# Two-layer hybrid encoder: a unit's transposes alternate on TensorE with the former unit's products with the values

## The chip, the cores and the metric

The kernel runs on one core of one Trainium2 chip. The metric is the time of one execution on the device in microseconds (us), the median of the runs. A profile of one execution comes with it; its times are us from the start of the span.

## What is computed

The reference is one step of a streaming encoder with two layers. Each layer adds to its input an output projection of three groups of heads side by side, and then an MLP. The first group is latent attention (MLA, 6 heads, each chunk of 64 frames sees all earlier chunks), the second a gated linear attention (GLA, 4 heads), the third attention over a band of chunks (6 heads, each chunk sees itself and the 8 before it). There are 1024 prompt frames and 8 running streams with 16 new frames each, 1152 columns in all; everything is float32.

```python
def _ca_prompt(q, k, v, table):
    ...
    s = jnp.einsum('bnqhe,bnkhe->bnhqk', qc, kb).astype(f32) * (E ** -0.5)
    ...
    p = jax.nn.softmax(s, axis=-1).astype(v.dtype)
    return jnp.einsum('bnhqk,bnkhe->bnqhe', p, vb).reshape(B, S, H * E)
...
for l in range(DEPTH):
    q, ckv, kr, gq, gk, gv, loga, g_out, cq, ck, cv = _project(_rmsnorm(xp, norm1[l]), pos_p, *proj_w)
    k_m, v_m = _mla_kv(ckv, kr, mla_w_kvup[l])
    o_mla = _mla_prompt(q, k_m, v_m)
    o_gla, S_fin = _gla_prompt(gq, gk, gv, loga)
    o_ca = _ca_prompt(cq, ck, cv, ca_rel_bias[l])
    xp = xp + _merge(o_mla, o_gla, g_out, o_ca, gla_out_norm[l], w_out[l])
    xp = xp + _mlp(_rmsnorm(xp, norm2[l]), w_up[l], w_down[l])
```

## The kernel before

A float32 value is kept as a high and a low part of a narrower type, and a product of two such values is made of up to three TensorE products (high by high, high by low, low by high). The dense projections work on columns in three groups of 384; each of their products is a "z" in the profile (128x384).

A layer runs through these stages (of layer 0, in us): norm and first input projections to 70; band attention 70 to 367; gated linear attention 367 to 545; latent attention 545 to 772; its sample part 772 to 810; norm, then the MLP 855 to 1618. Layer 1 repeats them: band attention 1688 to 1985, latent attention 2163 to 2385. In the attention stages two streams are merged. The primary stream is the attention; the dense stream, called the filler here, is the rest of the input projection and parts of the output projection. `drive()` (L358) takes from the one or the other in proportion to their costs, which each generator yields as it goes, so that TensorE has dense products while other engines do the softmax. The primary stream is emitted at a higher priority. From what is emitted, a scheduler sets the order on each engine by its own estimate of when operands are ready; the filler's products have scheduling-only dependencies on each other (`fq`, L58 to L63), which tie an order and wait for nothing at run time.

The function that the change touches is `attention()` (L395), which both attention stages use. Its unit is one head and two query tiles of 128, `a` = 0 and 1. For each query tile:

- `s_step` (L399) makes the scores with `mm` (L57) in one or two banks "s", takes the row maximum on DVE (L408), the exponent on ACT (L413) and normalises on DVE (L417). In band attention the operands of a score have 64 partitions ("64*128" in the profile, kH and qH), in latent attention 96.
- `t_step` (L420) runs three query tiles behind (`lag`). It transposes the probabilities on TensorE (`tr`, L72) block by block, up to four blocks of 128x128 into a bank "tp" (tile `ptp`). ACT copies the bank to the high part of a tile PT (L151), and DVE subtracts that from the bank to make the low part (L135). A bank is free once DVE has read it. PT tiles of the first four key blocks have two buffers, those of the later ones have one. GpSimd clears blocks that only one of the query tiles sees (L433).
- `pv_step` (L450) comes once for a unit, after both query tiles: it multiplies the values by all PT tiles into a bank "pv", first all high parts, then all low ones, in the order of the key blocks, up to 16 products in a row (128x256 each). ACT copies the bank out and the result is stored.

The loop at the end of `attention()` emits for each query tile its scores, then the whole `pv_step` of a unit that is pending, then the `t_step` of the query tile three behind. The eight PSUM banks are cut as d 2, s 2, tp 2, pv 2 in band attention, and d 2, s 3, tp 2, pv 1 in latent attention ("d" holds the filler's products).

## Time and profile before

| what | value |
|---|---|
| median of 3 runs | 3263.82 us (3259.57 to 3268.15) |
| profiled execution, its span | 3266.2 us |
| TensorE (PE) busy | 3137.7 us, 96% |
| VectorE (DVE), ScalarE (ACT), GpSimd (POOL) busy | 56%, 36%, 27% |
| span of a band attention stage, of a latent one | 297 us; 227 us (layer 0), 222 us (layer 1) |

For the profiled execution the span is its own time; it lies within the spread of the three runs. A row of a timeline has the start, the time from the first instruction's start to the last one's end, engine, line, operation, the tile written and the tiles read, shapes, and how many alike follow each other. Matmuls are pipelined, so the time of one row overlaps the next: the pace is read from start to start. The windows view gives the busy time of each engine in a stretch. PEld is TensorE's loading of the stationary operand.

### The profile page before, as it was taken

The numbers are of one execution on the slowest core, as the hardware profiler recorded it, in microseconds if no ns is written. First come the engines' busy times: TensorE is split into PE (matmuls) and PEld (weight loads), VectorE is DVE, ScalarE is ACT, GpSimd is POOL, SyncE is SP. The second block draws the span as 40 slices with busy tenths as digits, with TensorE's granted clock in tenths as the row PEclk, the third lists the DMA queues.
The fourth block names the chain that finished last, engine by engine and source line by source line (L and its number), as shares of the span: only waits on it lengthen the run. The fifth ranks groups of instructions, "written<-read, shape, count | busy, mean of one in ns | idle before, by whom it ended". The sixth has DMA issues, their size and how long they took to land.

```text
span 3266.2 us, 49236 instructions
## 1 busy us (share of the span) xinstructions
PE 3137.7 (96%) x18652; PEld 2982.4 (91%) x18652; DVE 1834.2 (56%) x3785; ACT 1190.6 (36%) x2781; POOL 866.1 (27%) x1122
## 2 busy tenths in 40 slices
PE   8999998998999999999999999889999999999998
PEld 7888887887999999999989888878889999999998
DVE  4554687885734434434555646978855443434436
ACT  4443454774311121111244434557743121111122
POOL 5221355443310010100242214654532010010112
PEclk9999999989999999999999999999999999999998
DMA  5232215224011111111143222142331111111111
GB/s 182 86 100 78 88 50 159 67 83 149 30 43 46 39 46 40 46 39 46 62 140 105 85 74 86 57 150 75 111 104 39 46 40 46 40 46 45 40 46 59
DMA packets 137612, 237.67 MB, mean 73 GB/s; under 512 B 16768, under 2 KB 105056, under 8 KB 137376
## 3 DMA queue, kind: packets, MB, share of 16 engines
q1 hardware_dynamic: 137376, 234.53, 22.3%
q8 instruction: 147, 2.41, 0.3%
q14 instruction: 89, 0.73, 0.1%
HBM read 178.64 MB, written 55.84 MB: 72 GB/s over the span
## 4 chain that ended last, share of the span: by engine, by line
PE 82%; DVE 9%; ACT 4%; issue 3%; DMA 1%; POOL 1%; SPq 0%; DVEq 0%; ACTq 0%; POOLq 0%
PE z L57 67%; PE s L57 4%; PE pv L57 3%; PE ptp L72 2%; PE rb L57 1%; DVE ga L743 1%; PE glao L57 1%; DVE mq L734 1%; PE lev L57 1%; DVE sbd L796 1%; ACT P L413 1%; DVE M L729 1%; PE ms L57 0%; DVE ng L408 0%; ACT PT L151 0%
## 5 line engine op out<-in xcount | busy, mean ns | idle before, releaser
L57 PE MATMUL z<-u,wdnh 128*128 128x384 f32 x3072 | 712.9, 334 | 0.1
L57 PEld LDWEIGHTS z<-u,wdnh 128*128 128x128 f32 x3072 | 548.6, 188 | 0.4 <-DVE u L135 0.4
L1253 DVE TENSOR_TENSOR x<-z,x 128x384 f32<-128x384 f32 x720 | 364.5, 551 | 288.0 <-PE z L57 288.0
L1227 POOL TENSOR_TENSOR relu<-relu 128x384 f32<-128x384 f32 x192 | 166.7, 895 | 1340.8 <-ACT u L1226 1336.1
L57 PE MATMUL z<-u,wdnl 128*128 128x384 f32 x1536 | 445.9, 334 | 0.0
L57 PE MATMUL z<-hH,wupl 128*128 128x384 f32 x1536 | 373.3, 334 | 0.0
L57 PE MATMUL z<-hL,wuph 128*128 128x384 f32 x1536 | 373.1, 334 | 0.0
L57 PE MATMUL z<-hH,wuph 128*128 128x384 f32 x1536 | 372.2, 334 | 0.0
L146 ACT ACTIVATE wdnh<-wdnr 128x1024 fp32r<-128x1024 f32 x64 | 68.0, 1062 | 686.4 <-PE z L57 686.4
L57 PEld LDWEIGHTS z<-u,wdnl 128*128 128x128 f32 x1536 | 282.3, 188 | 0.0
L57 PEld LDWEIGHTS z<-hH,wupl 128*128 128x128 f32 x1536 | 275.8, 188 | 0.0
L57 PEld LDWEIGHTS z<-hL,wuph 128*128 128x128 f32 x1536 | 275.8, 188 | 0.0
L57 PEld LDWEIGHTS z<-hH,wuph 128*128 128x128 f32 x1536 | 275.7, 188 | 0.0
L146 ACT ACTIVATE wuph<-wupr 128x1024 fp32r<-128x1024 f32 x64 | 68.0, 1062 | 514.6 <-PE z L57 512.6
L135 DVE TENSOR_TENSOR wdnl<-wdnr,wdnh 128x1024 fp32r<-128x1024 f32 x64 | 78.1, 1221 | 302.7 <-ACT wdnh L146 302.7
L135 DVE TENSOR_TENSOR wupl<-wupr,wuph 128x1024 fp32r<-128x1024 f32 x64 | 78.2, 1221 | 205.8 <-ACT wuph L146 205.8
L413 ACT ACTIVATE P<-s,ng 128x320 f32<-128x320 f32 (+5 forms) x288 | 157.4, 552 | 85.8 <-DVE ng L410 59.1
L135 DVE TENSOR_TENSOR u<-relu,u 128x384 fp32r<-128x384 f32 x192 | 148.9, 801 | 50.9 <-POOL relu L1227 50.9
L135 DVE TENSOR_TENSOR PT<-ptp,PT 128x512 fp32r<-128x512 f32 (+3 forms) x288 | 146.0, 518 | 52.6 <-ACT PT L151 44.3
L151 ACT ACTIVATE PT<-ptp 128x512 fp32r<-128x512 f32 (+3 forms) x288 | 127.3, 460 | 126.1 <-PE ptp L72 116.5
L72 PE MATMUL ptp<-ident,P 128*128 128x128 f32 x792 | 139.9, 283 | 15.2 <-DVE PT L135 12.0
L408 DVE TENSOR_REDUCE ng<-s 128x1 f32<-128x320 f32 (+5 forms) x288 | 146.7, 516 | 7.0 <-PE s L57 2.7
(416 smaller groups left out, 6447.5 us busy)
## 6 DMA issues: line engine op xcount, KB each, us to landing
wupr<-in_w_up_dram SPq DMA_DIRECT2D x64, 512.0 KB, 3.3
wdnr<-in_w_down_dram SPq DMA_DIRECT2D x64, 512.0 KB, 3.3
zs_dram<-z SPq DMA_DIRECT2D x102, 192.0 KB, 1.9
wo1r<-in_w_out_dram SPq DMA_DIRECT2D x48, 320.0 KB, 3.0
of<-os_dram SPq DMA_DIRECT2D x48, 192.0 KB, 3.5
xpart_dram<-xo SPq DMA_DIRECT2D x48, 192.0 KB, 1.9
xo<-xpart_dram SPq DMA_DIRECT2D x48, 192.0 KB, 3.5
cf<-zs_dram SPq DMA_DIRECT2D x36, 192.0 KB, 4.3
```

The lines of the kernel that those rows point to most:

```text
L57: i = T.matmul(*a, **k).ins
L72: T.transpose(out, in_, idn)
L135: eng.tensor_tensor(lo, src, h.bitcast(F32), ALU.subtract)
L146: S.activation(h, raw, AF.Copy)
L151: S.activation(o, i, AF.Copy, scale=scale)
L408: V.tensor_reduce(ng[:, x:x + 1], sc[x][:, :hi - lo], AX.X, ALU.max, negate=True)
L413: S.activation(pr[:, lo:hi], sc[x][:, :hi - lo], AF.Exp, bias=ng[:, 0:1], accum_out=ss[:, x:x + 1])
L729: V.tensor_tensor(mv[:, :, 0, :], mv[:, :, 0, :], kv[:, :, 0, :], ALU.mult)
L734: (GP if h else V).tensor_tensor(q2[hr, h, :w // 2].rearrange("p (n s) -> p n s", s=s), mv[hr, :, 1, :], qv[hr, :, 1, :], ALU.mult)
L743: V.copy_predicated(o, mk.to_broadcast([P, 2 * nt, 64 // s, s]), src)
L1227: GP.tensor_tensor(r, r, r, ALU.mult)
L1253: V.tensor_tensor(x[:, gsl(g)], o, x[:, gsl(g)], ALU.add)
```

## The change

Three things change in `attention()` and the helpers under it; no instruction is added or removed.

First, `pv_step` becomes a generator that stops after each product, and its products come in another order: the last four key blocks first, then the four before them; within four blocks all high parts, then all low ones.

Second, `t_step` calls `between()` ahead of each transpose, which emits the next product or products of the former unit. Under the first query tile these are half of the unit's products, under the second the rest, spread over the transposes. Before the next unit's generator starts, what is left of the former is emitted.

Third, transposes and products emitted in this way are tied to one another, each to the one before it, by a scheduling-only dependency (`behind`), so that the scheduler keeps them in this alternating order on TensorE.

```diff
+    def behind(i):
+        if chain:
+            tc.add_manual_dep(i, chain[0], NOSYNC, reason="order")
+        chain[:] = [i.name]
...
     def mm(*a, **k):
         i = T.matmul(*a, **k).ins
+        if linked[0]:
+            behind(i)
...
     def tr(out, in_, idn):
-        T.transpose(out, in_, idn)
+        i = T.transpose(out, in_, idn).ins
+        if linked[0]:
+            behind(i)
...
-            def t_step(u, a, pr):
+            def t_step(u, a, pr, between):
...
                     for i in range(n):
+                        linked[0] = True
+                        between(a, u.nk(a) - j - i)
                         tr(tp[:, i * P:(i + 1) * P], pr[:, (j + i) * P:(j + i + 1) * P], ident)
+                        linked[0] = False
...
             def pv_step(u):
                 po = bank("pv", "pv")
-                for w in range(2):
-                    for j in range(u.nj):
-                        mm(po[:, :256], u.v(u.jlo + j), u.pt[j // 4][w][:, j % 4, :],
-                           start=(w == 0 and j == 0), stop=(w == 1 and j == u.nj - 1))
+                todo = [(j, w) for x in reversed(range(0, u.nj, 4)) for w in range(2) for j in range(x, min(x + 4, u.nj))]
+                for i, (j, w) in enumerate(todo):
+                    mm(po[:, :256], u.v(u.jlo + j), u.pt[j // 4][w][:, j % 4, :],
+                       start=i == 0, stop=i == len(todo) - 1)
+                    if i < len(todo) - 1:
+                        yield
...
+            pend = [None, 0, 0]
+            def advance(n):
+                for _ in range(n):
+                    if pend[0] is not None:
+                        pend[1] -= 1
+                        if next(pend[0], "end") == "end":
+                            pend[0] = None
+            def between(a, left):
+                n = pend[1] if a else pend[1] - pend[2]
+                advance(-(-n // left))
+            def t_and_pv():
+                u, a, pr = todo.pop(0)
+                n = pend[1]
+                yield from t_step(u, a, pr, between)
+                yield (n - pend[1]) * 109
+                if a == 1:
+                    yield pend[1] * 109
+                    advance(99)
+                    pend[:] = [pv_step(u), 2 * u.nj, u.nj]
...
                     todo.append((u, a, s_step(u, a)))
                     yield u.nk(a) * P * u.npass / 2.4
-                    if pend is not None:
-                        pv_step(pend)
-                        yield pend.nj * 218
-                        pend = None
                     if len(todo) > lag:
-                        yield from t_step(*todo[0])
-                        if todo[0][1] == 1:
-                            pend = todo[0][0]
-                        todo.pop(0)
+                        yield from t_and_pv()
```

The lines of the file move with it: `mm` stands at L65 after, `tr` at L82.

On TensorE, in band attention of layer 0, at the second unit of the first pair of heads, before: `s` are scores from kH, kL, qH and qL, `pv` the products with values `cvhl`, `z` the filler.

```order
L57 MATMUL s_1869<-kH_1454,qH_1452 128x256
L57 MATMUL s_1869<-kL_1455,qH_1452 128x256
L57 MATMUL s_1869<-kH_1454,qL_1453 128x256
L57 MATMUL pv_1722<-PT_1693,cvhl_773 128x256
L57 MATMUL pv_1722<-PT_1693,cvhl_774 128x256 x2
L57 MATMUL pv_1722<-PT_1695,cvhl_774 128x256 x2
L57 MATMUL s_1881<-kH_1454,qH_1452 128x256
L57 MATMUL s_1881<-kL_1455,qH_1452 128x256
L57 MATMUL s_1881<-kH_1454,qL_1453 128x256
L57 MATMUL z_1913<-hH_380,win15h_1741 128x384
```

The same place after (`ptp` are the transposes of P):

```order
L65 MATMUL pv_1656<-PT_1573,cvhl_774 128x256
L82 MATMUL ptp_1711<-ident,P_1566 128x128
L65 MATMUL pv_1656<-PT_1573,cvhl_774 128x256
L82 MATMUL ptp_1711<-ident,P_1566 128x128
L65 MATMUL s_1869<-kH_1444,qH_1442 128x256
L65 MATMUL s_1869<-kL_1445,qH_1442 128x256
L65 MATMUL s_1869<-kH_1444,qL_1443 128x256
L65 MATMUL s_1881<-kH_1444,qH_1442 128x256
L65 MATMUL s_1881<-kL_1445,qH_1442 128x256
L65 MATMUL s_1881<-kH_1444,qL_1443 128x256
L65 MATMUL z_1913<-hH_380,win15h_1724 128x384
```

Before, two blocks of scores stood apart with five products between them; after, the products stand among the transposes ahead, and the six scores are one block.

On TensorE, at the end of latent attention of layer 0, before (`mvhl` are its values; the last products are those of the last unit):

```order
L72 MATMUL ptp_8758<-ident,P_8656 128x128 x4
L57 MATMUL pv_8733<-PT_8705,mvhl_7543 128x256 x4
L72 MATMUL ptp_8765<-ident,P_8656 128x128 x3
L57 MATMUL pv_8733<-PT_8707,mvhl_7986 128x256 x2
L72 MATMUL ptp_8771<-ident,P_8683 128x128 x4
L72 MATMUL ptp_8778<-ident,P_8683 128x128 x4
L57 MATMUL pv_8785<-PT_8752,mvhl_7543 128x256 x4
L57 MATMUL pv_8785<-PT_8754,mvhl_7986 128x256 x4
L57 MATMUL pv_8785<-PT_8753,mvhl_7543 128x256 x4
L57 MATMUL pv_8785<-PT_8755,mvhl_7986 128x256 x4
```

The same place after:

```order
L65 MATMUL pv_8740<-PT_8690,mvhl_7531 128x256
L82 MATMUL ptp_8759<-ident,P_8683 128x128
L65 MATMUL pv_8740<-PT_8690,mvhl_7531 128x256
L82 MATMUL ptp_8759<-ident,P_8683 128x128
L65 MATMUL pv_8740<-PT_8690,mvhl_7531 128x256
L82 MATMUL ptp_8770<-ident,P_8683 128x128
L65 MATMUL pv_8740<-PT_8690,mvhl_7531 128x256
L82 MATMUL ptp_8770<-ident,P_8683 128x128 x3
L65 MATMUL pv_8785<-PT_8735,mvhl_7974 128x256 x4
L65 MATMUL pv_8785<-PT_8736,mvhl_7974 128x256 x4
L65 MATMUL pv_8785<-PT_8733,mvhl_7531 128x256 x4
L65 MATMUL pv_8785<-PT_8734,mvhl_7531 128x256 x4
```

The second half of the former unit's products now stands one by one among the last eight transposes, and the last unit's own products begin with the key blocks whose PT tiles are written last.

More of the change, by code (lines that the diff above doesn't have):

```diff
@@ L54, in nm @@
         return f"{s}_{uid[0]}"
+    def behind(i):
+        if chain:
+            tc.add_manual_dep(i, chain[0], NOSYNC, reason="order")
+        chain[:] = [i.name]
+    chain = []
     def mm(*a, **k):
         i = T.matmul(*a, **k).ins
+        if linked[0]:
+            behind(i)
         if infill[0]:
@@ L63, in mm @@
             fq.append(i.name)
-    infill, fq = [False], []
+    infill, fq, linked = [False], [], [False]
     SQ_POOL = ((5, 7), (2, 5, 7))
@@ L473, in attention @@
                     yield u.nk(a) * P * u.npass / 2.4
-                    if pend is not None:
-                        pv_step(pend)
-                        yield pend.nj * 218
-                        pend = None
                     if len(todo) > lag:
-                        yield from t_step(*todo[0])
-                        if todo[0][1] == 1:
-                            pend = todo[0][0]
-                        todo.pop(0)
+                        yield from t_and_pv()
             while todo:
-                if pend is not None:
-                    pv_step(pend)
-                    yield pend.nj * 218
-                    pend = None
-                yield from t_step(*todo[0])
-                if todo[0][1] == 1:
-                    pend = todo[0][0]
-                todo.pop(0)
-            pv_step(pend)
-            yield pend.nj * 218
+                yield from t_and_pv()
+            yield pend[1] * 109
+            advance(99)
         def v_split(dst, src):
```

## The prediction

> **What bounds the kernel now.** I read the page first (busy times, then the chain that ended last), then the windows view for the stages, and only then single rows.
>
> ```profile
> span 3266.2 us, 49236 instructions
> PE 3137.7 (96%) x18652; PEld 2982.4 (91%) x18652; DVE 1834.2 (56%) x3785; ACT 1190.6 (36%) x2781; POOL 866.1 (27%) x1122
> PE 82%; DVE 9%; ACT 4%; issue 3%; DMA 1%; POOL 1%; SPq 0%; DVEq 0%; ACTq 0%; POOLq 0%
> ```
>
> TensorE (PE) is busy for 96% of the span and holds 82% of the chain. So a change can gain in two ways only: TensorE gets through its work at a better pace, or it waits less. The windows view tells where each is possible. The rows are chunk-band attention of layer 0, latent attention of layer 0, and the same two stages of layer 1; the columns after the window are busy times, then TensorE's granted clock.
>
> ```profile
> core 0: us, PE busy (x) PEld busy (x) DVE busy (x) ACT busy (x) POOL busy (x), PEclk, DMA share, GB/s
> 70.00:367.00 297.00, 295.56 (x1792) 262.38 (x1792) 157.69 (x416) 129.24 (x345) 67.22 (x121) 1.00 0.28 92
> 545.00:772.00 227.00, 201.37 (x1187) 181.22 (x1186) 180.02 (x436) 161.47 (x417) 112.25 (x144) 0.92 0.33 100
> ...
> 1688.00:1985.00 297.00, 295.56 (x1792) 262.39 (x1792) 158.10 (x416) 129.44 (x345) 67.31 (x121) 1.00 0.28 91
> 2163.00:2385.00 222.00, 198.59 (x1193) 178.16 (x1193) 177.45 (x434) 160.68 (x414) 110.21 (x144) 0.95 0.33 101
> ```
>
> The diff reaches the four attention stages alone. In chunk-band attention TensorE never rests (295.56 of 297.00), so only its pace counts there. In latent attention it rests 25.63 us in layer 0 and 23.41 in layer 1, at a clock of 0.92 and 0.95, so waits count there too. What the transposes wait for most in those two stages:
>
> ```profile
> PE ptp L72 <- DVE PT L135: 6.1, 5, 1.9
> ...
> PE ptp L72 <- DVE PT L135: 6.0, 5, 1.9
> ```
>
> The first row is of layer 0, the second of layer 1 (us in total, times, longest): a transpose needs a "tp" bank back, and DVE's subtraction is the last reader of it; 6.1 us in five waits.
>
> **The change part by part. Pace, transposes alternating with products.** Counted over the whole order, runs of transposes grow from 288 to 659, so there are 371 more places where a transpose stands alone next to a product. Before has a few such places by chance:
>
> ```profile
> 344.52 0.27 PE L72 MATMUL ptp<-ident,P 128*128 128x128 f32 x1
> 344.55 0.37 PE L57 MATMUL pv<-PT,cvhl 128*128 128x256 f32 x1
> 344.76 0.27 PE L72 MATMUL ptp<-ident,P 128*128 128x128 f32 x1
> 344.78 0.36 PE L57 MATMUL pv<-PT,cvhl 128*128 128x256 f32 x1
> 344.98 0.34 PE L57 MATMUL z<-hL,win7h 128*128 128x384 f32 x1
> ...
> 364.81 1.47 PE L57 MATMUL pv<-PT,cvhl 128*128 128x256 f32 x11
> 366.11 0.51 PE L57 MATMUL z<-hH,win9h 128*128 128x384 f32 x2
> ```
>
> Two alternated pairs take 344.98 - 344.52 = 0.46 us, 0.23 a pair. Apart, a product takes (366.11 - 364.81)/11 = 0.118, and a transpose in a run 0.11 (from the run of five below: 0.47 us to the next product, of which I put some 0.03 down to the last step). 0.118 + 0.11 = 0.228. So alternating saves nothing; it costs 0 to 0.010 us a pair. I take the middle, 0.005: 371 x 0.005 = **+1.9** (0 to +3.7). [...]
>
> **Pace, the score blocks.** Chunk-band scores use 64 partitions, and switching to them costs time:
>
> ```profile
> 116.47 0.34 PE L57 MATMUL z<-hH,win17l 128*128 128x384 f32 x1
> 116.74 0.41 PE L57 MATMUL s<-kH,qH 64*128 64x320 f32 x1
> 116.99 0.31 PE L57 MATMUL s<-kL,qH 64*128 64x320 f32 x1
> 117.14 0.31 PE L57 MATMUL s<-kH,qL 64*128 64x320 f32 x1
> 117.28 0.30 PE L57 MATMUL s<-kH,qH 64*128 64x320 f32 x1
> 117.43 0.30 PE L57 MATMUL s<-kL,qH 64*128 64x320 f32 x1
> 117.57 0.30 PE L57 MATMUL s<-kH,qL 64*128 64x320 f32 x1
> 117.81 0.44 PE L57 MATMUL z<-hH,win17h 128*128 128x384 f32 x1
> 118.09 0.34 PE L57 MATMUL z<-hL,win17h 128*128 128x384 f32 x1
> 118.27 0.33 PE L57 MATMUL z<-hH,win17l 128*128 128x384 f32 x1
> 118.44 0.34 PE L57 MATMUL z<-hH,win17h 128*128 128x384 f32 x1
> 118.61 0.71 PE L72 MATMUL ptp<-ident,P 128*128 128x128 f32 x5
> 119.08 0.42 PE L57 MATMUL z<-hL,win17h 128*128 128x384 f32 x1
> ```
>
> Undisturbed, a filler product (z) starts every 0.173 us (118.09 to 118.61 is three) and a score every 0.146 (116.99 to 117.57 is four). From 116.47 to 118.44 stand four z and six scores: 4 x 0.173 + 6 x 0.146 = 1.57 us, but 1.97 went by. One block costs 0.40 us beside its products, however many it holds. The order of after has fewer blocks, since products no longer stand in one lump between the scores of two query tiles: 68 + 68 become 59 + 55, 22 fewer: 22 x 0.40 = **-8.8**. If only one side of a block that merges is saved, it is half, -4.4. The other narrow products (the sample's scores and its products with the values, with 32 and 64 columns) come to two blocks more, which I put at **+0.5**, at most 2 x 0.40. These stages sum to -8.8 + 0.5 + 1.9 = **-6.4**. Nothing there can hide it or give it back, since TensorE rests 1.4 us in each.
>
> **Waits in latent attention.** Here the order matters in two places. The first is the end of the stage, where the dense filler has run out:
>
> ```profile
> 545.30:745.30 200.00, 180.65 (x1069) 163.60 (x1069) 160.23 (x390) 142.57 (x370) 104.34 (x130) 0.93 0.31 94
> 745.30:771.60 26.30, 20.02 (x116) 16.91 (x115) 19.79 (x46) 18.26 (x46) 7.35 (x14) 0.87 0.48 147
> ```
>
> After the last filler product before has 40 transposes, 56 products and 18 scores, 14.7 us at full pace (40 x 0.11, 56 x 0.118, and the scores at their 0.2 us), and takes 26.3: 0.56 us of work per us. The 200 us ahead hold 142 us of work by the same paces, 0.71. After has 57, 71 and 33 behind its last filler product, 20.8 us: the fillers are used up sooner, and 6.1 us of work move to where TensorE starves. 6.1/0.56 - 6.1/0.71 = 2.3 us a layer, **+4.6** for both. The lower bound is 0 (the moved work fills holes that are there anyhow), the upper one is in the rival below.
>
> The second is the body of the stage. A "tp" bank of four transposes is filled in 0.44 us before; with a product behind each it takes 0.93, which leaves ACT and DVE more time to empty the other bank. They need 0.54 + 0.61 us:
>
> ```profile
> L151 ACT ACTIVATE PT<-ptp x72: 258/537/599, 577.4 to 767.8; 128x512 fp32r<-128x512 f32 x36, 128x128 fp32r<-128x128 f32 x12, 128x256 fp32r<-128x256 f32 x12, 128x384 fp32r<-128x384 f32 x12
> L135 DVE TENSOR_TENSOR PT<-ptp,PT x72: 270/612/693, 578.2 to 768.6; 128x512 fp32r<-128x512 f32 x36, 128x128 fp32r<-128x128 f32 x12, 128x256 fp32r<-128x256 f32 x12, 128x384 fp32r<-128x384 f32 x12
> ```
>
> The brackets at the end of a row of the timeline give the rest ahead of it:
>
> ```profile
> 758.78 0.85 PE L72 MATMUL ptp<-ident,P 128*128 128x128 f32 x6 [0.69 <-DVE PT L135]
> ...
> 763.06 0.63 PE L72 MATMUL ptp<-ident,P 128*128 128x128 f32 x4 [0.99 <-DVE PT L135]
> ...
> 766.63 1.12 PE L72 MATMUL ptp<-ident,P 128*128 128x128 f32 x8 [1.89 <-DVE PT L135]
> ```
>
> Of the 6.1 us that transposes wait, these three lie in the tail; the other 2.5 lie in the body. I take half of that back, since the chain now also makes a transpose wait for the product before it, and that product for its PT tile: 2 x -1.2 = **-2.4** (-5.0 to 0). The new waits queue what stands behind them on TensorE (scores of the next units and filler), and DVE's row maximum waits for those scores; with filler at hand that costs nothing, in the tail it costs what the rival says.
>
> **The sum.** -6.4 + 4.6 - 2.4 = **-4.2**. The profiled execution has a span of 3266.2 us, 2.4 above the median of the runs, 3263.82, and inside their spread (3259.57 to 3268.15), so I take the sum off the median: **3259.6 us**. A difference of 0.3%, 9.8 us, is about what a measurement of this kernel can tell from no change; the forecast lies within it.
>
> **The rivals.** *The bank waits go altogether.* If the slower filling of banks takes away all waits of transposes for DVE, in the tail too, 6.1 + 6.0 = 12.1 us go in place of the +4.6 - 2.4: -6.4 - 12.1 = -18.5, **3245.3 us**. For it: 0.93 us of filling against 1.15 of emptying shared by two banks. Against it: the longest wait (1.89) stands where the next transposes have no products left to alternate with. Chance 0.25.
>
> *The clock stays up.* The half-clock stretches of 3.41 us come behind starved ones:
>
> ```profile
> 648.37:651.78 3.41, 2.29 (x16) 1.78 (x14) 3.22 (x9) 2.64 (x7) 1.99 (x2) 1.00 0.00 0
> 750.77:754.18 3.41, 1.61 (x14) 1.37 (x13) 3.41 (x8) 3.34 (x8) 1.18 (x2) 1.00 0.75 218
> 754.18:757.60 3.42, 3.42 (x15) 3.09 (x13) 2.17 (x6) 2.31 (x7) 1.52 (x2) 0.50 0.94 296
> ```
>
> If a transpose left the clock starved where a product feeds it, alternating would keep it up: five such stretches in both layers follow transposes, 17.1 us at half clock, and at most half of that is lost, 8.5: 3245.3 - 8.5 = **3236.8**. [...] Against it stands the first row, 16 matmuls busy 2.29 us with seven transposes among them, after which the clock held at full; what the second row has is 1.8 us of rest. Chance 0.05.
>
> *The tail locks up.* Transposes and products of the last units hang in one chain in the tail. There, by the order, the places where a bank is wanted again with under 2.1 us of TensorE work between (bank time 1.15 plus the hand-overs) go from nine to fourteen, and their shortage from 6.0 to 10.1 us: +4.1. The one "pv" bank is wanted 0.5 us sooner at three places, some +0.7, and the first product now reads the group of PT that was written last, +0.6. That is 5.4 a layer, 10.8 for both. Starved longer, the clock falls for two more stretches a layer, 4 x 1.7 = 6.8. With -6.4 from the pace: +11.2, **3275.0 us**, slower. It decides once the tail grows past 26.3 + 8 us a layer. Against it: the tail's waits before are of ACT and DVE, which do no more work than before. Chance 0.16.
>
> *The change does nothing*: merged score blocks save nothing, because what costs the 0.40 us moves elsewhere, and the moved filler costs what the body gains; then +1.9 of the pairs is left, 3265.7 us, part of "the same".
>
> **How the numbers follow.** The forecast and the case of no effect hold 0.54; the two faster ones 0.25 + 0.05 = 0.30; slower 0.16. The range runs from 3242 (the first rival with the pair term at 0, 3243.4, and a share of the second) to 3276 (above the third). Faster by over 0.3% means under 3254.0: 0.30; within: 0.54; slower, over 3273.6: 0.16.
>
> **What would show it.** Right: chunk-band windows shorter by some 3.2 us each, with TensorE busy throughout; alternated pairs at 0.23 us; the filler-less tail of latent attention longer than 26.3 us and the body shorter. Wrong: chunk-band windows unchanged (no price on blocks), rows of transposes waiting for DVE gone from the waits (first rival), or the same rows grown past 10 us in a layer with new half-clock stretches (third).

## The result and the profile after

The changed kernel takes 3298.24 us (median of 4 runs, 3293.24 to 3299.6), the kernel before 3264.89 (4 runs, 3259.57 to 3268.15): the ratio is 1.0097, with a 95% interval of 1.0084 to 1.0109. It is 33 us slower, where no measurable change was forecast. The profiled execution of after is the fastest of its four, so the two traces differ by less, 25.3 us of span. The page of after, the first lines:

```profile
span 3291.5 us, 49166 instructions
PE 3146.8 (96%) x18652; PEld 2990.8 (91%) x18652; DVE 1842.9 (56%) x3785; ACT 1193.4 (36%) x2781; POOL 870.9 (26%) x1122
```

Shares of the span say nothing here: TensorE is 96% busy in both. The stages do. In the windows view, cut at the first and last products of each stage, layer 0 of before (band attention; GLA up to the first query product of latent attention; latent attention up to its last filler product; from there to its last product with the values; the rest up to the MLP):

```profile
73.38:366.02 292.64, 291.20 (x1767) 258.27 (x1767) 156.71 (x416) 126.54 (x340) 65.70 (x120) 1.00 0.28 89
366.02:562.56 196.54, 177.50 (x1161) 157.93 (x1159) 161.08 (x341) 101.78 (x245) 107.21 (x131) 0.93 0.32 102
562.56:745.01 182.45, 165.31 (x981) 149.51 (x982) 147.61 (x372) 134.19 (x354) 94.16 (x118) 0.93 0.28 84
745.01:771.40 26.39, 20.11 (x116) 16.97 (x116) 19.98 (x47) 18.55 (x46) 7.15 (x14) 0.87 0.48 146
771.40:828.56 57.16, 53.56 (x329) 49.30 (x328) 26.98 (x49) 20.65 (x47) 16.32 (x24) 1.00 0.39 118
```

The same five stretches of after, and band attention of its layer 1 (292.65 us before):

```profile
74.63:375.36 300.73, 297.33 (x1767) 264.30 (x1767) 160.84 (x416) 127.50 (x339) 65.44 (x119) 0.97 0.27 86
375.36:569.16 193.80, 175.75 (x1160) 156.09 (x1159) 160.09 (x340) 101.87 (x244) 109.02 (x131) 0.94 0.33 104
569.16:745.86 176.70, 157.41 (x934) 139.79 (x935) 140.38 (x354) 129.07 (x340) 88.88 (x110) 0.96 0.27 81
745.86:785.50 39.64, 29.31 (x163) 24.57 (x163) 27.00 (x65) 24.21 (x60) 12.25 (x22) 0.83 0.33 106
785.50:844.73 59.23, 54.98 (x329) 50.68 (x329) 26.81 (x48) 20.77 (x46) 16.35 (x24) 0.97 0.40 122
1708.54:2004.08 295.54, 290.80 (x1767) 262.36 (x1767) 161.93 (x416) 127.13 (x340) 65.97 (x119) 0.98 0.27 89
```

Band attention is 8.1 us longer (2.9 in layer 1), GLA 2.7 shorter. Latent attention shows the forecast's picture in a larger size: 5.8 us shorter up to the last filler product (981 matmuls become 934) and 13.3 longer behind it (116 become 163); in layer 1 it is 7.9 shorter and 15.2 longer. The rest is 2.1 longer.

Where the time of a stretch goes can be estimated from the starts of all matmuls. From each one to the next, the undisturbed pace of its kind is work; what the row shows as rest is rest; what lies in a stretch of half clock is clock; what is left is put down to switching between kinds. For band attention, in us:

| stage | work | rest | clock | switching |
|---|---|---|---|---|
| layer 0 before / after | 260.1 / 260.1 | 1.4 / 3.4 | 0.0 / 7.4 | 31.1 / 29.8 |
| layer 1 before / after | 260.1 / 260.1 | 1.4 / 4.7 | 0.0 / 4.3 | 31.1 / 26.4 |

Switching became 6.0 us cheaper in the two stages, close to the 6.4 that the pace terms had. But the clock took 11.7 and rest 5.3, and both were forecast as nothing. In band attention of layer 0 the clock was halved twice for 6.83 us; of a third stretch at half clock, from 373.4 on, 2 us lie in the stage. Windows ahead of and in these stretches, of after:

```profile
182.25:185.66 3.41, 2.40 (x11) 1.53 (x11) 2.93 (x10) 2.24 (x8) 0.20 (x1) 1.00 0.00 0
185.66:192.49 6.83, 6.83 (x22) 5.75 (x21) 3.55 (x12) 2.07 (x7) 0.20 (x1) 0.50 0.13 41
305.13:308.54 3.41, 3.41 (x35) 2.54 (x35) 0.00 (x0) 0.02 (x1) 0.58 (x2) 1.00 0.52 173
308.54:315.37 6.83, 6.83 (x23) 4.94 (x23) 2.65 (x7) 1.35 (x3) 0.20 (x1) 0.50 0.04 13
```

The first fall follows a window with rest, 2.40 us busy; the window from 648.37 in the prediction, 2.29 us busy, kept its clock. The second follows no rest: TensorE is busy for all of 305.13 to 308.54. What it does there, in the timeline of after (start, time, tile; `caso` are the sample's products with the values, in narrow form, 128*64):

```profile
304.78 1.13 PE L65 MATMUL caso<-ptc,vc 128*64 128x16 f32 x18
...
306.08 0.38 PE L65 MATMUL pv<-PT,cvhl 128*128 128x256 f32 x1
306.39 0.29 PE L65 MATMUL caso<-ptc,vc 128*64 128x16 f32 x2
306.61 0.33 PE L82 MATMUL ptp<-ident,P 128*128 128x128 f32 x1
306.87 0.29 PE L65 MATMUL caso<-ptc,vc 128*64 128x16 f32 x2
307.09 0.38 PE L65 MATMUL pv<-PT,cvhl 128*128 128x256 f32 x1
307.40 0.29 PE L65 MATMUL caso<-ptc,vc 128*64 128x16 f32 x2
307.62 0.33 PE L82 MATMUL ptp<-ident,P 128*128 128x128 f32 x1
```

The products of 16 columns are cut up by tied transposes and products, two at a time. From 306.08 to 307.62 stand three pairs of them and three single ones in 1.54 us, of which 0.69 is their pace (six at 0.058, two products at 0.118, one transpose at 0.109): the other 0.85 us come to 0.14 for each of the six switches. There is no filler between, and of these 1.54 us less than half is the products' own pace, though by the profile TensorE never rests.

In latent attention the wait that the first rival wanted gone did go for the most part: transposes waited 6.1 us for DVE before and wait 1.4 after. Others took its place. Waits of TensorE in layer 0 up to the last filler product, before:

```profile
PE s L57 <- ACT P L413: 3.5, 5, 1.3
PE ptp L72 <- DVE PT L135: 2.5, 2, 1.6
...
PE q L57 <- DVE rq L955: 2.1, 1, 2.1
```

and after:

```profile
PE q L65 <- DVE rq L983: 5.9, 5, 2.9
PE s L65 <- ACT P L425: 4.5, 7, 1.6
```

Behind the last filler product, before:

```profile
PE ptp L72 <- DVE PT L135: 3.6, 3, 1.9
PE pv L57 <- ACT PT L151: 2.0, 2, 1.8
PE s L57 <- ACT P L413: 0.4, 1, 0.4
```

and after:

```profile
PE s L65 <- ACT P L425: 5.5, 3, 2.4
PE pv L65 <- ACT PT L163: 3.0, 3, 1.4
PE ptp L82 <- DVE PT L147: 1.4, 2, 1.1
```

Over the whole stage scores now wait 10.0 us for a score bank, which ACT's exponent has to give back (3.8 before). Most of the growth stands behind the last filler product. Ahead of it, where filler is at hand, it is the query products' wait for DVE that grew. DVE and ACT wait longer too. Waits of DVE and of ACT in latent attention, before:

```profile
DVE PT L135 <- ACT PT L151: 3.2, 6, 0.9
ACT PT L151 <- PE ptp L72: 7.8, 13, 2.0
```

and after:

```profile
DVE PT L147 <- ACT PT L163: 12.1, 16, 2.6
ACT PT L163 <- PE ptp L82: 12.6, 15, 1.8
```

DVE stands 12.1 us in front of its PT subtraction for the copy that ACT makes first, and ACT stands 12.6 us in front of that copy for the transposes of the bank. In the program's order the next exponents and row maxima can stand behind these. But ACT's exponents did not wait longer for row maxima: 13.7 us against 15.5 before. And the two longest waits of scores behind the last filler product, 2.35 us (until 756.94) and 2.23 (until 765.45), end with exponents that stand on ACT behind other work: the splitting of an MLP weight (`wuph`) and of a head's output that is loaded back (`oH`), each with a wait for its load:

```profile
754.37 1.06 ACT L158 ACTIVATE wuph<-wupr 128x1024 fp32r<-128x1024 f32 x1 [0.49 <-DMA wupr<-in_w_up_dram]
...
763.81 1.02 ACT L163 ACTIVATE oH<-of 128x384 fp32r<-128x384 f32 x2 [2.18 <-DMA of<-os_dram]
```

### The profile page after: what moved, and what is told of

It reads as the page before. It is cut to its first block, busy times and chain, and to the rows that moved or that the text cites. A ratio compares the mean times of both kernels' runs of the same rounds, so it can differ in the third digit from the quotient of the medians.

```text
span 3291.5 us, 49166 instructions
## 1 busy us (share of the span) xinstructions
PE 3146.8 (96%) x18652; PEld 2990.8 (91%) x18652; DVE 1842.9 (56%) x3785; ACT 1193.4 (36%) x2781; POOL 870.9 (26%) x1122
## 4 chain that ended last, share of the span: by engine, by line
PE 66%; DVE 6%; ACT 3%; issue 2%; DMA 2%; POOL 1%; SPq 0%; DVEq 0%; ACTq 0%; POOLq 0%
PE z L65 57%; PE s L65 2%; PE pv L65 2%; PE ptp L82 1%; DVE PT L147 1%; PE rb L65 1%; ACT P L425 1%; ACT PT L163 0%; DMA of<-os_dram 0%; PE ms L65 0%; PE glao L65 0%; DMA wo1r<-in_w_out_dram 0%; ACT ob L163 0%; DVE ga L771 0%; DVE ng L420 0%
## 5 line engine op out<-in xcount | busy, mean ns | idle before, releaser
L65 PE MATMUL z<-u,wdnh 128*128 128x384 f32 x3072 | 712.8, 334 | 0.1
L65 PEld LDWEIGHTS z<-u,wdnh 128*128 128x128 f32 x3072 | 548.7, 188 | 0.4 <-DVE u L147 0.4
L65 PE MATMUL z<-u,wdnl 128*128 128x384 f32 x1536 | 445.9, 334 | 0.0
L65 PE MATMUL z<-hL,wuph 128*128 128x384 f32 x1536 | 373.3, 334 | 0.0
L65 PE MATMUL z<-hH,wupl 128*128 128x384 f32 x1536 | 373.3, 334 | 0.0
L65 PE MATMUL z<-hH,wuph 128*128 128x384 f32 x1536 | 372.2, 334 | 0.0
L65 PEld LDWEIGHTS z<-u,wdnl 128*128 128x128 f32 x1536 | 282.3, 188 | 0.0
L65 PEld LDWEIGHTS z<-hL,wuph 128*128 128x128 f32 x1536 | 275.8, 188 | 0.3
L65 PEld LDWEIGHTS z<-hH,wupl 128*128 128x128 f32 x1536 | 275.9, 188 | 0.0
L65 PEld LDWEIGHTS z<-hH,wuph 128*128 128x128 f32 x1536 | 275.7, 188 | 0.0
L147 DVE TENSOR_TENSOR PT<-ptp,PT 128x512 fp32r<-128x512 f32 (+3 forms) x288 | 145.3, 516 | 103.7 <-ACT PT L163 90.0
L82 PE MATMUL ptp<-ident,P 128*128 128x128 f32 x792 | 185.5, 283 | 5.4 <-DVE PT L147 5.2
L446 POOL MEMSET PT<- 128x128 f32 x240 | 50.3, 219 | 418.2 <-PE pv L65 334.6
```

Of the source, the lines that this page charges most:

```text
L65: i = T.matmul(*a, **k).ins
L82: i = T.transpose(out, in_, idn).ins
L147: eng.tensor_tensor(lo, src, h.bitcast(F32), ALU.subtract)
L446: GP.memset(q[:, j % 4, aa * P:(aa + 1) * P].bitcast(F32), 0.0)
```

## The experiments

**One stage at a time.** The attention of before is kept as a second function, `attention0`, and called for the one or the other stage.

```diff
-            for cost in attention(units(), mp, 8 * P, 4, 3):
+            for cost in attention0(units(), mp, 8 * P, 4, 3):
```

> Alternation in the band attention alone; latent attention emitted as before. Theory A (the pace came as forecast, but stretches without filler let TensorE rest and its clock fall): in the profile after, the two band stages are 7.8 and 3.0 us longer and the two GLA stages behind them 2.6 and 4.5 us shorter, so about +4 us, 3269 us, with half-clock stretches inside the band stages. Rival B (an alternated pair costs TensorE more than the rows said): 171 of the 371 added places lie here, so 171/371 of the 33 us, +15 us, 3280 us, and pairs above 0.23 us. Rival C (the loss lies in latent attention alone): the forecast pace of band attention, -6 us, 3259 us.

3276.96 us against 3264.92, ratio 1.0033 (1.0022 to 1.0043). Theory A named the stage rightly, with half-clock stretches in it (10.2 and 6.8 us in layer 0), but the size was 12 us, not 4. The estimate came from a profiled execution that lay at the low end of its runs, which may be part of it.

```diff
-                        yield from attention(units(), ap, 5 * P, 2, 3)
+                        yield from attention0(units(), ap, 5 * P, 2, 3)
...
-                        yield from merge(attention(units(), ap, 5 * P, 2, 3), ca_sample(ap, box))
+                        yield from merge(attention0(units(), ap, 5 * P, 2, 3), ca_sample(ap, box))
```

> Alternation in latent attention alone; band attention emitted as before. Theory A: the part behind the last filler product grows from 26 to 40 us a layer and the part ahead of it shrinks by 6, +7.4 a layer and some 1.5 behind the stage: +18 us, 3283 us. Rival B (pairs): 198 of 371 places, +18 us too, but then by pairs above 0.23 us and with the rest of TensorE unchanged, which the profile tells apart. Rival C: the whole +33 us, 3298 us.

3285.0 us, ratio 1.0064 (1.0046 to 1.0082): 20 us, as theory A had it. The two stages sum to 32 of the 33 us, so nothing shows that they act on each other. An alternated pair takes 0.231 us in the median in both stages of after, and 0.232 where band attention has such pairs before, so rival B falls in both.

**The tie.**

```diff
     def behind(i):
-        if chain:
-            tc.add_manual_dep(i, chain[0], NOSYNC, reason="order")
         chain[:] = [i.name]
```

> Products and transposes are emitted in alternation as after, but not tied: the scheduling-only dependencies between them are left out. By the order there are then 149 runs of transposes a layer (144 before, 329 after), 60 and 59 blocks of band scores (68 before), and 121 matmuls behind the last filler of latent attention (114 before, 161 after). Theory A: the tie is what pushes filler away from the waits; without it 3264.9 - 17 x 0.3 = about 3260 us, and no half-clock stretch in the band stages. Rival D (the new emission order and the reversed order of the products do it, not the tie): it stays near 3290 us or above.

3283.99 us, ratio 1.0067 (1.0041 to 1.0093): some 14 us of the 33 go with the tie, 19 stay (13 to 30 by the interval). Theory A's 3260 is wrong and rival D is nearer: emission and product order alone cost most of it, with 149 runs of transposes, nearly as few as before. The half-clock stretches in band attention, which theory A put down to the tie, are there without it too: 10.2 and 3.4 us in each layer.

**The filler of latent attention.**

```diff
-            drive(mla_stream(open_pool(stack, "mla")), 165e3, 5 * 8 * STEP)
+            drive(mla_stream(open_pool(stack, "mla")), 165e3, 4.0 * 8 * STEP)
```

> After, but in latent attention the filler is spread by a share of 4.0 in place of 5 (the divisor in the drive call), so that it lasts longer: by the order 71 matmuls stand behind the last filler product in place of 161. Theory A: the tail of 40 us loses its starved part, the body gives up some filler: 5 to 10 us less a layer, 3298 - 15 = about 3283 us. Rival E (the waits of latent attention come from the tied order itself, wherever the filler stands): the tail shortens and the body lengthens by the same, 3298 us within 4.

3300.93 us, ratio 1.011 (1.0092 to 1.0128). The part behind the last filler shrank from 39.6 to 17.3 us as intended, the part ahead grew from 176.7 to 188.8, and the stage behind grew by 8. In sum it is as rival E says: the rest moves with the filler. Latent attention itself got shorter, by 10.0 us in layer 0 and 4.4 in layer 1. The stage behind lost it again: the 20 dense products that had opened it come behind the sample's first scores here, and its clock is at half for 13.7 and 17.1 us (3.4 and 0 in after).

The same in the kernel with alternation in latent attention alone, with a share of 4.4, which leaves less filler over:

> Alternation in latent attention alone, with the filler spread by a share of 4.4 in place of 5: 126 matmuls behind the last filler product (161 without that, 114 before), and no filler left over for the stage behind. Theory K: the loss of latent attention is in the starved part, which falls from 40 to about 30 us while the part ahead grows by 5: 3285 - 10 = 3275 us. Rival E (the rest moves with the filler and stays in sum): 3285 us within 4.

3300.05 us, ratio 1.011 (1.0093 to 1.0127), 15 us more than without the shift, where theory K wanted 10 less. In layer 0 latent attention itself kept its time (215.2 us against 215.6), with 30.7 us behind the last filler product in place of 40.1; the loss is behind it, 65.0 us against 59.0, with the clock at half for 10.2 us against 3.4. Since both runs take dense products from the start of the next stage, they don't settle what the starved part alone costs. Waits of this kernel in that stretch:

```profile
PE mss L65 <- DMA kcm<-in_mla_ckvT_dram: 2.7, 1, 2.7
```

The sample's first scores stand there for their load, the largest of these waits; what else makes this stretch longer was not taken apart.

**By banks.** The products stand ahead of a bank's transposes in one run, not between them.

```diff
+                    linked[0] = True
                     for i in range(n):
-                        linked[0] = True
                         between(a, u.nk(a) - j - i)
+                    for i in range(n):
                         tr(tp[:, i * P:(i + 1) * P], pr[:, (j + i) * P:(j + i + 1) * P], ident)
-                        linked[0] = False
+                    linked[0] = False
```

> As after, but alternation by banks: ahead of a bank's transposes stand all the products that after puts between them, and then the transposes in one run; order of the products and ties stay. Theory F (in latent attention ACT and DVE work in order and stand waiting for a bank that fills at half the rate, while row maxima and exponents of the scores wait behind; TensorE then waits for score banks): DVE's rest ahead of the PT subtraction in latent attention of layer 0 falls from 12.6 us back towards 3.7, the wait of scores for the exponent from 10.1 towards 3.9, and the time by some 5 us a layer: 3288 us. Rival G (the spread of the products over the next unit does it, at whatever grain): within 4 us of 3298.

3282.17 us against 3266.89, ratio 1.0055 (1.0033 to 1.0076): 16 us less than after. The time fell by more than theory F's 10 us, but its rows did not come: DVE's rest ahead of all PT subtractions of the span fell only from 103.7 to 97.4 us (52.6 before), in latent attention of layer 0 from 12.6 to 10.2 and not to 3.7, and the scores of latent attention still waited 8.0 and 9.2 us. So banks that fill more slowly were not the whole story.

> Alternation by banks in latent attention alone; band attention as before. In the run with alternation by banks everywhere, latent attention took 208.8 and 208.2 us (before 208.7 and 204.8, after 216.3 and 212.1). Theory M (one by one costs latent attention some 6 us a layer more than by banks): 3285 - 12 = 3273 us. Rival: that run's gain was in where the clock fell by chance, 3285 us within 4.

3275.15 us against 3264.8, ratio 1.0021 (1.0005 to 1.0036): theory M holds. In latent attention alone, with the new order of the products in both, one by one costs 20 us and by banks 10.

**The order of the products.**

```diff
-                for w in range(2):
-                    for j in range(u.nj):
-                        mm(po[:, :256], u.v(u.jlo + j), u.pt[j // 4][w][:, j % 4, :],
-                           start=(w == 0 and j == 0), stop=(w == 1 and j == u.nj - 1))
+                todo = [(j, w) for x in reversed(range(0, u.nj, 4)) for w in range(2) for j in range(x, min(x + 4, u.nj))]
+                for i, (j, w) in enumerate(todo):
+                    mm(po[:, :256], u.v(u.jlo + j), u.pt[j // 4][w][:, j % 4, :],
+                       start=i == 0, stop=i == len(todo) - 1)
```

> Before, with only the new order of a unit's products (last four key blocks first, high and low parts together). Theory A and F: no part in the loss; five blocks of band scores fewer a layer, so 3264.9 - 4 = 3261 us, within 4. Rival I (the first product waits for the PT tile that is written last): the wait of products for ACT's PT copy grows by 0.5 us in each of 24 units a layer, 24 us, 3289 us.

3277.31 us against 3266.89, ratio 1.0028 (1.0012 to 1.0044): the order alone, with nothing alternating, costs 10 us. Theories A and F missed it; rival I had the direction, but more than twice the size.

> Before, with the new order of a unit's products in latent attention alone; nothing alternates. Theory N (the order is a cause of its own: the last unit's first product reads the PT tile that is written last, and products wait for it): as in the run with the new order in both attentions, the part behind the last filler grows by some 3 us a layer, 3265 + 7 = 3272 us. Rival: the 10 us of that run lay in band attention, 3265 us within 3.

3280.1 us against 3265.1, ratio 1.0045 (1.0029 to 1.006). Theory N has the direction, and the loss is twice its size. The part behind the last filler went from 26.4 to 30.0 us in layer 0, as theory N said. But the part ahead of it got 2.7 us shorter there, and most of the loss in this trace lies in layer 1 (5.0 us ahead of the last filler product, 5.3 behind it). One trace says little of such sizes: in the five traces here whose latent attention is emitted as before, the stage took 203.8 to 212.1 us in layer 0 and 201.9 to 208.1 in layer 1, with 13.7 to 34.1 us of it at half clock. Two figures are steadier in these ten stages: TensorE's rest, 22.2 to 24.9 us (27.0 and 25.5 with the new order, 29.6 and 28.3 in after), and the wait for score banks, 3.0 to 4.5 us. Waits of the kernel with the new order from latent attention of layer 0 to the MLP:

```profile
PE s L57 <- ACT P L413: 7.4, 10, 1.5
PE pv L57 <- ACT PT L151: 6.1, 4, 2.7
```

Products wait 6.1 us for ACT's PT copies (3.2 before), and scores 7.4 for their banks (3.8 before): the same longer wait as after, without any alternation.

**The old order under alternation.** With two buffers for the later PT tiles the old order can be kept.

```diff
-                        u.pt.append([ap.tile([P, ny if x else 4, 256], F32R, tag=f"PT{x // 4}{y}", name=nm("PT"), bufs=1 if x else 2)
+                        u.pt.append([ap.tile([P, ny if x else 4, 256], F32R, tag=f"PT{x // 4}{y}", name=nm("PT"), bufs=2)
...
-                todo = [(j, w) for x in reversed(range(0, u.nj, 4)) for w in range(2) for j in range(x, min(x + 4, u.nj))]
+                todo = [(j, w) for w in range(2) for j in range(u.nj)]
```

> Alternation by banks in latent attention alone (3275 us with the new order of the products), with the old order: all high parts, then all low ones, for which the PT tiles of the later key blocks have two buffers in place of one. 146 matmuls behind the last filler product (152, 114 before). Theory N: the part that is due to the order goes, 3275 - 7 = 3268 us. Rival O (the order costs nothing once products stand among the transposes): 3275 us within 3.

3270.11 us, ratio 1.0016 (1.0007 to 1.0025): 5 us less than by banks with the new order, between N and O, though the intervals of the two ratios overlap. Two things changed together, the order and the buffers; the new order with two buffers was not run. The wait of scores is back where it was before:

```profile
PE q L65 <- DVE rq L1084: 5.2, 4, 2.0
PE s L65 <- ACT P L425: 3.8, 5, 1.6
```

> Alternation one by one in latent attention alone (3285 us with the new order), with the old order of the products and two buffers for all PT tiles; 143 matmuls behind the last filler product. Theory N: 3285 - 7 = 3278 us. Rival P (the single buffer of the later PT tiles is what makes products and transposes wait for each other): more, 3285 - 15 = 3270 us. Rival O: 3285 us within 3.

3284.65 us, ratio 1.007 (1.0054 to 1.0085), the same as one by one with the new order. Its scores wait as long as there:

```profile
PE s L65 <- ACT P L425: 8.7, 11, 1.8
```

So either of the two lengthens the wait for score banks, one by one or the new order, and having both is no worse than the first. With two buffers the 20 us stay, so single buffers (rival P) are not their cause.

**The last head as before.**

```diff
-                        linked[0] = True
-                        between(a, u.nk(a) - j - i)
+                        linked[0] = not u.plain
+                        if not u.plain:
+                            between(a, u.nk(a) - j - i)
...
+                if u.plain:
+                    todo = [(j, w) for w in range(2) for j in range(u.nj)]
...
+                if u.plain:
+                    m = pend[1]
+                    advance(99)
+                    yield m * 109
...
+                            u.plain = (p, h) == (2, 1)
                             yield u
```

> Alternation in latent attention alone, for the first five heads; the last head, four units that make up most of what stands behind the last filler product, is emitted as before. By the order 161 matmuls still stand behind the last filler product (161 with all six heads, 114 before). Theory K (what costs is filler used up too soon): the part behind the last filler stays at 37 to 40 us, 3285 us within 4. Rival L (what costs is tied alternation where there is no filler): that part falls to 20.7 us of work at before's 0.56, 34 to 37 us, the waits of scores for the exponent halve, 3277 us.

3278.07 us against 3264.8, ratio 1.0038 (1.0025 to 1.0052). The time is rival L's. The 37.2 us behind the last filler in layer 0 fit both, and scores still wait 6.6 us, not half of the 8.6 with all six heads. With the same 161 matmuls behind the last filler, some 7 us of the 20 are gone, so the new order of the last head costs beyond the work that moved there. Where it costs is not shown: behind the last filler product the trace has 2.8 us less in layer 0 and 0.2 more in layer 1.

**Band attention, the third pair.** Only the third pair has the sample's products merged into it. With the attention of before for that pair:

```diff
-                        yield from merge(attention(units(), ap, 5 * P, 2, 3), ca_sample(ap, box))
+                        yield from merge(attention0(units(), ap, 5 * P, 2, 3), ca_sample(ap, box))
```

> Alternation in the first two pairs of heads of band attention alone; the third pair, into which the sample's products are merged, and latent attention are emitted as before. Theory A: against alternation in all three pairs (3277 us) the half-clock stretch behind the sample's products goes, 3.4 us a layer, and the stretch without filler at the start of the second pair stays: 3270 us. Rival C2 (the loss of band attention lies at the start of the second pair alone): within 3 us of 3277.

3260.65 us against 3266.89, ratio 0.9994 (0.9979 to 1.001). The whole loss of band attention comes with the third pair, and it is more than the 7 us expected. The third pair gets back its old order of the products here as well as its old emission. More runs of the same kernel:

> The kernel with alternation in the first two pairs of band attention alone, once more with more runs: it is the one that came out below before (3260.7 against 3266.9). If the pace term is what is left there (11 and 7 blocks of scores fewer, 0.40 us each, and some 135 alternated pairs at 0.005 us): 18 x 0.40 - 0.7 = 6.5 us under before. If its low median was chance: within 2 us of before.

3261.48 us against 3265.1, ratio 0.999 (0.9982 to 0.9999): 3.6 us under before, little more than half of the pace term. It is the one version here below the kernel before. The two traces of this kernel also show what the stretch at the start of the second pair costs: in layer 1 the first has no stretch at half clock and takes 289.96 us, the second has one of 6.8 us there, from 1801.2 on, and takes 292.65.

**Fewer stops.** The merged streams take a step at each stop of the generator; here the stops are as many as there are banks.

```diff
                 n = pend[1]
-                yield from t_step(u, a, pr, between)
-                yield (n - pend[1]) * 109
+                for c in t_step(u, a, pr, between):
+                    yield c + (n - pend[1]) * 109
+                    n = pend[1]
```

> As after, with fewer stops of the generator: the products' cost is added to the stop of each bank of transposes in place of stops of its own. The merged streams (a head's queries and keys in latent attention, the sample's products in band attention) take one step at each stop, so they are spread as before; by the order the sample's products with the values then stand in 4 runs a layer (8 before, 13 and 8 after). Theory H (these steps came too close together in after): the wait of q for DVE's rq in latent attention falls from 5.9 and 4.7 to about 2 us, and the half-clock stretch behind the sample's products in band attention goes: 3 us in each, 3298 - 12 = 3286 us. Rival G: within 4 us of 3298.

3293.82 us against 3266.89, ratio 1.0085 (1.0063 to 1.0107). The wait of q fell to 2.9 and 1.4 us and the stretch near 300 us went, as theory H said; the time fell by 4, not 12. TensorE's rest from the start of latent attention to the MLP did not fall in layer 0 (38.2 us; 33.9 in after). Band attention takes 294.2 us in both layers (300.7 and 295.5 in after).

> Alternation in all three pairs of band attention, latent attention as before, with fewer stops of the generator, so that the sample's products stand in 4 and 9 runs a layer. Theory A2 (the third pair costs because the sample's narrow products are cut up between tied transposes and products, and the clock falls there): in layer 0, where the runs are 4, no half-clock stretch near 300 us, the stage near 294 us; about 3266 us against 3277 with alternation in all three pairs and the stops of after. Rival J (the third pair costs because it alternates at all): 3277 us within 3, the half-clock stretch near 300 us stays.

3270.42 us against 3264.8, ratio 1.002 (1.0008 to 1.0032). The time lies between theory A2's 3266 and rival J's 3277. The two layers of this one kernel are the cleanest test. In layer 0 the sample's products stand in four runs:

```profile
296.71 1.13 PE L65 MATMUL caso<-ptc,vc 128*64 128x16 f32 x18
...
300.20 0.41 PE L65 MATMUL caso<-ptn,cvs 128*64 128x128 f32 x2
300.54 0.39 PE L65 MATMUL pv<-PT,cvhl 128*128 128x256 f32 x1
300.77 0.27 PE L82 MATMUL ptp<-ident,P 128*128 128x128 f32 x1
```

In layer 1 they are cut into pairs as after. The two band stages:

```profile
74.00:368.28 294.28, 290.69 (x1767) 259.84 (x1767) 160.65 (x416) 127.43 (x340) 65.71 (x120) 0.99 0.28 89
1691.23:1989.44 298.21, 294.35 (x1767) 264.34 (x1767) 160.24 (x416) 127.32 (x340) 66.21 (x120) 0.98 0.28 88
```

Layer 0 has no half-clock stretch at the sample's products and takes 294.28 us; layer 1 has one of 3.41 us there and takes 298.21. A stretch of 3.41 us at half clock loses at most 1.7, so not all of the 3.9 us is due to it: part of it is another stretch at the end of the stage. Over the traces the stages go with the cutting up: 294.2 to 294.3 us with four runs of the sample's products (three stages), 300.7 to 301.4 with 13 runs (three stages that alternate one by one). That is as theory A2 has it. But cutting up is not the only way to the fall: with only the new order, and once with alternation in two pairs, the clock fell behind the sample's products (from 301.6 and 303.4 on, 3.4 us) though they stood in one run.

## Why the prediction was wrong

**Pace of alternated pairs: right.** The timeline of after, in band attention:

```profile
108.02 0.27 PE L82 MATMUL ptp<-ident,P 128*128 128x128 f32 x1
108.04 0.36 PE L65 MATMUL pv<-PT,cvhl 128*128 128x256 f32 x1
108.25 0.27 PE L82 MATMUL ptp<-ident,P 128*128 128x128 f32 x1
...
108.70 0.27 PE L82 MATMUL ptp<-ident,P 128*128 128x128 f32 x1
```

From 108.02 to 108.70 stand three pairs: 0.68 us, 0.227 each, against 0.228 apart. Alternation is neutral to TensorE's pace here; the median pair, 0.231, is within the forecast's 0 to 0.010 us.

**Price of score blocks: right in sum.** Switching in the band stages fell by 1.3 and 4.7 us, 6.0 in all, where blocks, samples and pairs together were put at 6.4. That the total fits is in part luck: the layers were put at equal shares. By the same reckoning it is 5.0 and 3.2 where the sample products are left alone (alternation in two pairs, 3260.65 us), so the cut-up sample products probably ate some of it in layer 0. Why a block of scores on 64 partitions costs 0.40 us beside its products, no run here shows.

**"Nothing there can hide it or give it back, since TensorE rests 1.4 us in each": wrong, the first of the two steps that failed.** It took a stage without rest for one that cannot lose, and so put clock and rest at nothing; in the trace of after they took 11.7 and 5.3 us. The new order made stretches without filler in the stage, with the tie and without it: one at the start of the second pair, and one at the sample's products, where the clock fell with no rest at all. At the first of them two rows of the timeline of after wait, and then the clock falls for 6.8 us:

```profile
182.74 0.44 PE L65 MATMUL s<-kH,qH 64*128 64x384 f32 x1 [0.75 <-ACT P L425]
...
184.37 0.51 PE L65 MATMUL pv<-PT,cvhl 128*128 128x256 f32 x2 [0.47 <-ACT PT L163]
```

Band attention alone cost 12 us against the 6 of gain that were forecast. The first stretch is the smaller part: it is there too when only two pairs alternate, at 2.7 us a stage (289.96 against 292.65), and that kernel is not slower than before. The rest comes with the third pair, and some 7 us of it with how the sample's products are cut up (301.40 against 294.28 us in layer 0). The pace gain shows only when the third pair is left out.

**The end of latent attention: the mechanism right, the sum far too small.** More work did move behind the last filler product, by the amount that the order showed. The sum had +10.9 us behind it, and -8.6 and -1.2 ahead of it, net 1.1 a layer. The trace of after shows +13.3 and -5.8 in layer 0 and +15.2 and -7.9 in layer 1, net 7.5 and 7.3; the run with latent attention alone has 20 us for both. The starved part ran at 20.8 us of work in 39.6, 0.53, not 0.56, and its clock was at half for 13.7 us (6.8 before). Moving the filler back did not help the kernel (two runs), but those runs starved the next stage instead, so whether the starved part is the cause of the loss or the place where it shows stays open.

**"The new waits ... with filler at hand that costs nothing": wrong, the second step that failed.** Ahead of the last filler product of layer 0, where filler is at hand, the transposes' waits went from 2.5 us to nothing, more than the half that was reckoned. It was no gain: queries wait 5.9 us there against 2.1 and scores 4.5 against 3.5, and TensorE rests 19.3 us against 17.1, with 47 matmuls fewer. Behind it, waits of scores grew from 0.4 to 5.5 us, a row for which the sum had nothing. The forecast weighed the "tp" banks alone. The order of the products was priced at 0.6 us a layer in the third rival and at nothing in the sum, and alone it costs 10 to 15 us in all.

**The rivals.** The third one, slower through the end of latent attention (3275 us), had the sign, and with 10.8 + 6.8 = 17.6 us nearly the size for that stage (20 us); its two more stretches at half clock a layer came (13.7 and 10.2 us behind the last filler in after, 6.8 and 3.4 before). Its transposes that wait longer did not come; scores wait in their place. It missed band attention, where it kept the forecast's gain. The second, that alternation keeps the clock up, has the sign wrong in band attention: TensorE's clock was at half there for 15.6 us of layer 0 and 9.4 of layer 1, and for none before. That a transpose does less for the clock than a product was a supposition of the author's; no run here shows it.

**What is left open.** That the wait for score banks lengthens is shown by runs for one-by-one alternation without the new order (8.7 us) and for the new order without alternation (7.4), the first with two buffers for the later PT tiles. How it does so was not tried by itself. That ACT and DVE stand longer at their PT rows (12.6 and 12.1 us) is an argument from the waits. Against it stand the two rows of ACT above, where other work and its loads hold up the exponents, and the run with the new order alone, where ACT waits 7.4 us for transposes, no longer than before (7.8). Some 5 us of latent attention by banks with the old order are not explained by a wait for score banks, nor by TensorE's rest in layer 0 (23.2 us, 23.4 before); queries waiting for DVE (5.2 us against 2.1) are the largest row left.

## What to carry to other kernels

A stage in which TensorE hardly rests can still be slowed by a new order (band attention of layer 0 had 1.4 us of rest and became 8.1 us longer): look for the stretches that lose their dense filler, and for narrow products that get cut up among single transposes. Where three engines pass banks to each other, cost the rows of all kinds of banks before a wait removed at one of them is booked as a gain: in latent attention of layer 0 the transposes' wait for DVE fell from 6.1 to 1.4 us, and the scores' wait for ACT grew from 3.8 to 10.0. And the order in which an accumulation reads its inputs is a change of its own, 10 to 15 us here: cost it by when the last of them is written.

## What the runs showed of the hardware

TensorE's clock was halved after a window of 3.41 us in which by the profile TensorE was busy for all of it, 35 matmuls of which 28 had 16 columns (the windows view above, 305.13 to 308.54). The busy time of the profile was no guide to the fall: the clock held behind a window of 3.41 us with 2.29 us busy in before (from 648.37), and fell behind one with 2.40 us busy in after (from 182.25). What decides was not found. With fewer stops, 6.80 us full of the same products in runs kept the clock (297.00 to 303.80, 85 matmuls, busy throughout). With only the new order, the clock fell behind 3.40 us busy throughout (298.20 to 301.60, 40 matmuls) in which these products stood in one run.
